# Attention values in one set of PSUM columns, and a softmax on negated scores

## The chip, the cores and the metric

One program on one core of a Trainium2 chip. The metric is the time of one execution on the device, in microseconds; lower is better. The core's engines work at the same time and wait for each other by semaphores: TensorE (PE) multiplies and writes to PSUM, VectorE (DVE) and ScalarE (ACT) compute on SBUF and PSUM, GpSimd (POOL) computes on SBUF and starts some transfers, SyncE (SP) starts the others.

## What is computed

One layer of an encoder, for a prompt of 2048 tokens and a sample of 8 x 16 tokens: a modulated RMS norm and a projection, a mixer of two halves (a gated delta rule, and attention in a band), an output projection and a feed-forward network. The change lies in the attention of the prompt, for 8 heads of width 64:

```
def one_chunk(c):                      # 64 queries, the 64 keys of their chunk and the 512 before them
    s = jnp.einsum('bqhd,bkhd->bhqk', qc, kc).astype(jnp.float32) * (DH ** -0.5) + bias
    p = jax.nn.softmax(jnp.where(valid, s, -jnp.inf), axis=-1).astype(v.dtype)
    return jnp.einsum('bhqk,bkhd->bqhd', p, vc)
```

and, in the softmax alone, in the attention of the sample.

## The kernel before

The kernel is written in a tile framework: the code says what is computed and in which buffers, pools hand out buffers of a tag in turn, and a scheduler sets the order of the instructions on each engine and their semaphores from the program as a whole. An edit in one place can so move instructions elsewhere.

Numbers are float32. For speed, the large matmuls run on fp32r operands; so that no accuracy is lost, an operand is split into two words, a high one (a rounded copy, by ACT) and a low one (the rest, by DVE or POOL), and their products are added. `mm3` (L160) does three matmuls for one product that way. The weights are cast by ACT (L175) and their low words made by POOL (L180) or loaded back from a store.

Phase 1 makes projections and the delta rule; the attention of token tiles 0 and 1 (`attention_first`) runs in it. Phase 2 takes the 16 token tiles and the sample tile in five blocks of 2, 4, 4, 4 and 3 tiles (`BLOCKS2`). For each block it runs `out_proj` (products `pso`), then `ffn`: 32 steps of `ffn_up` (products `psu`, L1480 to L1482; relu and square on ACT; the square again and the low word of `u` on DVE) and after every fourth the products `psd` with w_down, which DVE adds to `y`. While a block is in its FFN, the attention of the next block (`attention_gen`, L1212) is put in as filler: `tick` counts matmul columns and takes a step of the generator when enough have gone by.

A step of `attention_gen` handles a unit, one head of one tile of 128 queries, in three places of a pipeline. `scores` multiplies the queries (two words, `Qt`, stationary) with the keys into `psS`. `softmax_to` adds the bias and takes the maximum in one DVE pass (L1113), negates the maximum (L1114), takes the exponential with a running sum on ACT (L1115, listed at L92), inverts the sum (L1116) and scales (L1117). `probs` transposes the probabilities by PE into `psP` (L1275) and splits them into two words in `PT` (L1277): `PT[:, a, 0]` is the high word and `PT[:, a, 1]` the low one of key tile a. `values` multiplies: the stationary operand is `KV[:, w0 + a, 1]`, 128 keys by 128 columns, of which 64 are the high and 64 the low word of V; the moving one is `PT[:, a]`, both words side by side, 256 columns. The result `pv` has the words of V in its two halves of partitions and those of the probabilities in its two halves of columns; ACT copies the lower half of partitions to `otmp` (L1287), DVE adds the upper one (L1288) and then adds the two halves of columns to `of` (L1290; both adds are listed at L82), and SP stores `of` (L1292). `pv` has one buffer, which it shares with `pq`, the transposed queries of `prep_q` (L1250). A tile has 3, 4 or 5 key tiles; 112 units have 536 together.

Of the kernel before, what the change touches and what calls it, by code (L numbers as in the profile page):

```python
# [8 lines left out]
F32 = mybir.dt.float32  # L9
F32R = mybir.dt.float32r  # L10
AF = mybir.ActivationFunctionType
ALU = mybir.AluOpType
AX = mybir.AxisListType.X

P = 128
# [16 lines left out]
NEG = -1.0e30  # L32
# [19 lines left out]
class Trunk:  # L52
# [1056 lines left out]
    def softmax_to(self, s, ps, bias):  # L1109
        nc = self.nc  # L1110
        sv = s if len(ps.shape) == 2 else s.rearrange("p (z c) -> p z c", z=2)
        sm = self.small.tile([P, 4], F32, tag="sm", name="sm", bufs=4)
        nc.vector.tensor_tensor_reduce(sv, ps, bias, 1.0, NEG, ALU.add, ALU.max, sm[:, 0:1])  # L1113
        self.ts(sm[:, 1:2], sm[:, 0:1], -1.0, ALU.mult)  # L1114
        self.act(s, s, AF.Exp, bias=sm[:, 1:2], accum_out=sm[:, 2:3])  # L1115
        nc.vector.reciprocal(sm[:, 3:4], sm[:, 2:3])  # L1116
        self.ts(s, s, sm[:, 3:4], ALU.mult)  # L1117

# [93 lines left out]
    def attention_gen(self, tiles):  # L1212

        nc = self.nc
        mm = nc.tensor.matmul
# [4 lines left out]
        ap, ap2 = self.ap, self.ap2  # L1220
        heads, Q = {}, {}

        def psum(name):
            if name in ("pv", "pq"):
                return ap2.tile([P, 512], F32, tag="pv", name=name, bufs=4 - GP)
            return ap2.tile([P, 1024], F32, tag="att", name=name, bufs=2)
# [28 lines left out]
        def span(t):  # L1255
            lo_t = max(0, t - 4)
            return t + 1 - lo_t, lo_t - k0
# [22 lines left out]
        def values(h, t, PT):  # L1280
            m, w0 = span(t)
            KV = heads[h][0]
            pv = psum("pv")
            for a in range(m):
                mm(pv[:, 0:256].rearrange("p (z t) -> p z t", z=2), KV[:, w0 + a, 1], PT[:, a], start=(a == 0), stop=(a == m - 1))  # L1285
            tm = ap.tile([64, 256], F32, tag="otmp", name="otmp", bufs=2)
            nc.scalar.copy(tm, pv[64:128, 0:256])  # L1287
            self.tt(tm, tm, pv[0:64, 0:256], ALU.add)  # L1288
            o = ap.tile([64, P], F32, tag="of", name="of", bufs=2)
            self.tt(o, tm[:, 0:P], tm[:, P:256], ALU.add)  # L1290
            u = h % 2
            nc.sync.dma_start(self.s_ob[t][u * 64:(u + 1) * 64, h // 2], o)  # L1292

# [15 lines left out]
        pr, PT = {}, {}  # L1309
        for i in range(len(units) + 3):  # L1310
            if i >= 3:
                h, t = units[i - 3]
                values(h, t, PT.pop(i - 3))
                if t == tiles[-1]:
                    load_k(h + 2)
            if 2 <= i < len(units) + 2:
                PT[i - 2] = probs(*units[i - 2], pr.pop(i - 2))
            if i < len(units):
                h, t = units[i]
                pr[i] = scores(h, t)  # L1320
                if qs is not None:
                    prep_q(*qs)
                qs = next_q() if h % 2 and todo else None
            yield
# [267 lines left out]
```

## Time and profile before

| | us |
|---|---|
| median of the timed runs (3) | 3242.33 |
| lowest and highest of them | 3240.86, 3249.45 |
| profiled execution | 3235.24 |
| its span, from first to last instruction | 3233.5 |
| PE busy | 3071.4 (95%) |
| weight loads busy | 2713.0 (84%) |
| DVE busy | 1903.2 (59%) |
| ACT busy | 1478.5 (46%) |
| POOL busy | 701.2 (22%) |
| mean granted TensorE clock | 0.977 |

The clock is given as a share of 2.4 GHz; the granted level at any moment is that or half of it, 1.2 GHz. A matmul's row in the trace runs from its start to the modelled end of its results, so consecutive ones overlap: what one costs PE is the distance from its start to that of the next. A weight load (PEld) has a row of its own. The shares are means over stretches with different limits, so stretches are read apart.

### The profile page before, as it was taken

To read this page: it belongs to the slowest core of one execution; us is meant where nothing else is said; L and a number is where in the kernel's file an instruction comes from. 1 tells how busy PE (TensorE), PEld (TensorE's weight loads), DVE (VectorE), ACT (ScalarE), POOL (GpSimd) and SP (SyncE) were. 2 spreads that over 40 slices of the span, in tenths; PEclk is the share of its full clock that TensorE was granted. 3 is DMA by queue.
4 is the path that set the end of the run, shared out by engine and by line. 5 is a ranking of instruction groups with operands and counts; after the bars stand their busy time and mean duration, and the time that the engine had idled before them with its cause. 6 is when DMAs were issued, how large, how long until landed. Compare 5 with 4: busy or idle time off the path is not lost.

```text
span 3233.5 us, 53068 instructions
## 1 busy us (share of the span) xinstructions
PE 3071.4 (95%) x19577; PEld 2713.0 (84%) x19577; DVE 1903.2 (59%) x4526; ACT 1478.5 (46%) x2707; POOL 701.2 (22%) x561
## 2 busy tenths in 40 slices
PE   7899999999999979988999999999999999998998
PEld 6798988899989968878888889888888887787997
DVE  5985777777868676888446567235455443243223
ACT  3554544556656555554424444344434443333332
POOL 4641312121222347653343320000000000000000
PEclk9999999999989999998999999999999999998999
DMA  9789896878888765565565666665676667677875
GB/s 298 225 264 283 269 288 207 266 236 245 282 292 262 223 201 167 160 222 174 170 200 188 204 214 228 195 195 186 204 246 191 209 230 230 222 239 224 258 246 195
DMA packets 624507, 730.71 MB, mean 226 GB/s; under 512 B 59040, under 2 KB 483088, under 8 KB 622200
## 3 DMA queue, kind: packets, MB, share of 16 engines
q1 hardware_dynamic: 618488, 695.87, 68.0%
q0 software_dynamic: 5760, 31.46, 3.0%
q8 instruction: 154, 2.52, 0.3%
q14 instruction: 105, 0.86, 0.1%
HBM read 614.57 MB, written 115.52 MB: 226 GB/s over the span
## 4 chain that ended last, share of the span: by engine, by line
PE 71%; DVE 12%; DMA 9%; issue 3%; ACT 2%; SPq 1%; POOL 1%; POOLq 0%; DVEq 0%; ACTq 0%
PE psd L164 7%; PE psd L162 7%; PE psu L1480 7%; PE psu L1481 7%; PE psd L163 7%; PE psu L1482 7%; PE pv L1285 2%; PE psq L521 2%; PE psq L520 2%; PE psq L519 2%; PE psb L162 2%; PE psb L164 2%; PE psb L163 2%; PE psS L1267 2%; PE pso L162 2%
## 5 line engine op out<-in xcount | busy, mean ns | idle before, releaser
L175 ACT CAST w<-raw 128x1024 fp32r<-128x1024 f32 (+1 forms) x528 | 552.7, 1048 | 349.2 <-PE psd L164 163.2
L82 POOL TENSOR_TENSOR w<-raw,w 128x1024 fp32r<-128x1024 f32 (+1 forms) x172 | 418.3, 2443 | 365.8 <-ACT w L175 327.5
L1480 PE MATMUL psu<-hT,w 128*128 128x512 f32 (+2 forms) x1304 | 468.6, 361 | 7.1 <-ACT hT L104 6.2
L1481 PE MATMUL psu<-hT,w 128*128 128x512 f32 (+2 forms) x1304 | 467.2, 359 | 1.2 <-DVE hT L82 1.2
L1482 PE MATMUL psu<-hT,w 128*128 128x512 f32 (+2 forms) x1304 | 465.7, 357 | 0.0
L164 PE MATMUL psd<-w,u 128*128 128x512 f32 x1088 | 431.4, 398 | 9.1 <-DVE u L82 9.1
L162 PE MATMUL psd<-w,u 128*128 128x512 f32 x1088 | 432.5, 398 | 7.9 <-DVE y L82 4.1
L163 PE MATMUL psd<-w,u 128*128 128x512 f32 x1088 | 427.6, 393 | 0.0
L82 DVE TENSOR_TENSOR r<-r 128x512 f32<-128x512 f32 (+2 forms) x160 | 178.8, 1117 | 399.7 <-ACT u L92 399.4
L82 DVE TENSOR_TENSOR y<-y,psd 128x512 f32<-128x512 f32 x238 | 162.2, 684 | 242.0 <-PE psd L164 241.4
L1480 PEld LDWEIGHTS psu<-hT,w 128*128 128x128 f32 x1304 | 246.6, 190 | 39.8 <-ACT hT L104 7.4
L1481 PEld LDWEIGHTS psu<-hT,w 128*128 128x128 f32 x1304 | 246.8, 189 | 33.2 <-DVE hT L82 2.3
L1482 PEld LDWEIGHTS psu<-hT,w 128*128 128x128 f32 x1304 | 246.6, 189 | 32.5 <-issue 0.2
L92 ACT ACTIVATE r<-psu 128x512 f32<-128x512 f32 (+2 forms) x160 | 85.5, 534 | 408.7 <-PE psu L1482 349.6
L164 PEld LDWEIGHTS psd<-w,u 128*128 128x128 f32 x1088 | 204.9, 189 | 56.7 <-DVE u L82 10.4
L162 PEld LDWEIGHTS psd<-w,u 128*128 128x128 f32 x1088 | 205.3, 189 | 53.5 <-DVE y L82 6.7
L163 PEld LDWEIGHTS psd<-w,u 128*128 128x128 f32 x1088 | 205.6, 189 | 45.4 <-issue 1.0
L162 PE MATMUL psb<-w,hT 128*128 128x256 f32 x816 | 236.3, 290 | 0.7 <-ACT qraw L976 0.7
L164 PE MATMUL psb<-w,hT 128*128 128x256 f32 x816 | 234.1, 288 | 0.5 <-DVE hT L82 0.5
L163 PE MATMUL psb<-w,hT 128*128 128x256 f32 x816 | 233.4, 287 | 0.0
L520 PE MATMUL psq<-hT,w 128*128 128x384 f32 (+1 forms) x576 | 194.1, 337 | 0.0
L521 PE MATMUL psq<-hT,w 128*128 128x384 f32 (+1 forms) x576 | 193.9, 337 | 0.0
(318 smaller groups left out, 6603.0 us busy)
## 6 DMA issues: line engine op xcount, KB each, us to landing
raw<-in_w_up_dram SPq DMA_DIRECT2D x160, 512.0 KB
raw<-in_w_down_dram SPq DMA_DIRECT2D x160, 512.0 KB
raw<-in_w_in_dram SPq DMA_DIRECT2D x156, 512.0 KB
w<-s_w_in SPq DMA_DIRECT2D x130, 512.0 KB
w<-s_w_up SPq DMA_DIRECT2D x96, 512.0 KB
w<-s_w_down SPq DMA_DIRECT2D x96, 512.0 KB
raw<-in_w_out_dram SPq DMA_DIRECT2D x40, 512.0 KB
x<-in_x_prompt_dram SPq DMA_DIRECT2D x38, 512.0 KB
```

The lines of the kernel that those rows point to most:

```text
L82: (eng or self.nc.vector).tensor_tensor(out, in0, in1, op)
L92: self.nc.scalar.activation(out, in_, func, **kw)
L162: mm(out, lh, rh, start=first, stop=False)
L163: mm(out, lh, rl, start=False, stop=False)
L164: mm(out, ll, rh, start=False, stop=last)
L175: nc.scalar.copy(w[:, 0, 0:n], r)
L519: mm(ps[:, 0:T], wh, hT[:, k, 0, 0:T], start=(k == 0), stop=False)
L520: mm(ps[:, 0:T], wh, hT[:, k, 1, 0:T], start=False, stop=False)
L521: mm(ps[:, 0:T], wl, hT[:, k, 0, 0:T], start=False, stop=(k == KT - 1))
L1480: mm(ps[:, c0:c1], wh, h2[:, k, 0, c0:c1], start=(k == 0), stop=False)
L1481: mm(ps[:, c0:c1], wh, h2[:, k, 1, c0:c1], start=False, stop=False)
L1482: mm(ps[:, c0:c1], wl, h2[:, k, 0, c0:c1], start=False, stop=(k == KT - 1))
```

## The change

In `values` of `attention_gen`, the one matmul for each key tile, with both words of the probabilities side by side, becomes two with 128 columns each, which accumulate into the same 128 columns of `pv`. The add of the two halves of columns and the buffer `otmp` go; the ACT copy and the remaining DVE add have half the columns, and write to `of`. `attention_first` keeps its form.

In `softmax_to`, which all attention uses, the DVE pass stores the negated sum of score and bias and takes its minimum, which is the negated maximum. The exponential takes the scale -1 and that minimum as its bias, and the instruction that negated the maximum goes.

```
-        nc.vector.tensor_tensor_reduce(sv, ps, bias, 1.0, NEG, ALU.add, ALU.max, sm[:, 0:1])
-        self.ts(sm[:, 1:2], sm[:, 0:1], -1.0, ALU.mult)
-        self.act(s, s, AF.Exp, bias=sm[:, 1:2], accum_out=sm[:, 2:3])
+        nc.vector.tensor_tensor_reduce(sv, ps, bias, -1.0, -NEG, ALU.add, ALU.min, sm[:, 0:1])
+        self.act(s, s, AF.Exp, scale=-1.0, bias=sm[:, 0:1], accum_out=sm[:, 2:3])
...
             for a in range(m):
-                mm(pv[:, 0:256].rearrange("p (z t) -> p z t", z=2), KV[:, w0 + a, 1], PT[:, a], start=(a == 0), stop=(a == m - 1))
-            tm = ap.tile([64, 256], F32, tag="otmp", name="otmp", bufs=2)
-            nc.scalar.copy(tm, pv[64:128, 0:256])
-            self.tt(tm, tm, pv[0:64, 0:256], ALU.add)
+                for z in range(2):
+                    mm(pv[:, 0:P], KV[:, w0 + a, 1], PT[:, a, z], start=(a + z == 0), stop=(a == m - 1 and z == 1))
             o = ap.tile([64, P], F32, tag="of", name="of", bufs=2)
-            self.tt(o, tm[:, 0:P], tm[:, P:256], ALU.add)
+            nc.scalar.copy(o, pv[64:128, 0:P])
+            self.tt(o, o, pv[0:64, 0:P], ALU.add)
```

The scheduler writes a new order for both engines. On PE, among the products with w_down of a block with four tiles, a unit of five key tiles stood so before:

```order
L1285 MATMUL pv<-PT,KV 128x256 x5
L162 MATMUL psd<-w,u 128x512
L163 MATMUL psd<-w,u 128x512
L164 MATMUL psd<-w,u 128x512
L1275 MATMUL psP<-ident,sS 128x128 x5
L1267 MATMUL psS<-KV,Q 128x384 x2
L1267 MATMUL psS<-KV,Q 128x256 x2
```

and such a unit now, where lines after the removed one have a number lower by one:

```order
L1285 MATMUL pv<-PT,KV 128x128 x10
L1274 MATMUL psP<-ident,sS 128x128 x5
L1266 MATMUL psS<-KV,Q 128x384 x2
L1266 MATMUL psS<-KV,Q 128x256 x2
L162 MATMUL psd<-w,u 128x512
L163 MATMUL psd<-w,u 128x512
```

The ten narrow matmuls stand in a row, with no other matmul between the two of a pair. Of 112 units, 75 have ten in one row; in others the first stands apart by a few rows.

On DVE, in the FFN of the first block (two tiles), where the attention of tiles 2 to 5 is filled in, a unit's output and another's softmax stood so before (ISA is the pass with the maximum and the read of its result, `r` and `u` belong to the FFN):

```order
L82 TENSOR_TENSOR otmp<-otmp,pv 64x256
L1113 ISA sS,sm<-psS,bias 128x640
L1113 ISA sm 128x1
L82 TENSOR_TENSOR PT<-psP,PT 128x4x128
L82 TENSOR_TENSOR of<-otmp 64x128
L87 TENSOR_SCALAR sm<-sm 128x1
L1116 RECIPROCAL sm<-sm 128x1
L87 TENSOR_SCALAR sS<-sS,sm 128x640
```

and now:

```order
L82 TENSOR_TENSOR of<-of,pv 64x128
L1113 ISA sS,sm<-psS,bias 128x640
L1113 ISA sm 128x1
L82 TENSOR_TENSOR PT<-psP,PT 128x4x128
L82 TENSOR_TENSOR y<-y,psd 128x512
L1115 RECIPROCAL sm<-sm 128x1
L87 TENSOR_SCALAR sS<-sS,sm 128x640
```

The add from `otmp` and the negation are gone from between the maximum and the inverted sum, and an add to `y` has moved up into their place.

## Rows read from the trace of the kernel before

**Rows 1.** Busy time by stretch: length, PE, PEld, DVE, ACT, POOL, clock, DMA share, GB/s
```profile
1127.00:1187.00 60.00, 44.66 (x295) 40.34 (x296) 40.39 (x98) 30.03 (x58) 26.99 (x24) 0.86 0.71 232
1187.00:1439.00 252.00, 227.12 (x1467) 202.19 (x1466) 200.08 (x295) 137.99 (x252) 157.77 (x81) 0.98 0.56 169
1439.00:1529.00 90.00, 74.30 (x553) 70.96 (x552) 73.49 (x154) 40.57 (x77) 26.56 (x19) 0.88 0.59 191
1529.00:1941.00 412.00, 408.59 (x1981) 340.71 (x1980) 227.44 (x360) 169.34 (x278) 152.92 (x83) 0.99 0.61 197
...
1998.00:2413.00 415.00, 413.01 (x2027) 345.74 (x2028) 181.79 (x390) 178.63 (x296) 7.98 (x25) 1.00 0.62 199
...
2464.00:2627.00 163.00, 159.79 (x829) 135.32 (x830) 79.65 (x185) 81.39 (x144) 6.13 (x19) 0.98 0.65 208
```

**Rows 2.** The same for L1285 alone, the value product: length, PE, PEld, clock, DMA
```profile
1127.00:1187.00 60.00, 3.53 (x17) 2.65 (x17) 0.86 0.71 232
1187.00:1439.00 252.00, 17.10 (x102) 14.42 (x102) 0.98 0.56 169
1439.00:1529.00 90.00, 9.61 (x42) 7.66 (x42) 0.88 0.59 191
```

**Rows 3.** Timeline of PE, a unit among w_down's products: start, us, instruction
```profile
1706.28 0.40 PE L164 MATMUL psd<-w,u 128*128 128x512 f32 x1
1706.52 0.75 PE L1285 MATMUL pv<-PT,KV 128*128 128x256 f32 x5
1707.10 0.75 PE L1267 MATMUL psS<-KV,Q 128*128 128x384 f32 x4
```

**Rows 4.** Timeline of PE, scores of the first attention, two 128 and two 256
```profile
1023.38 0.62 PE L1163 MATMUL psS<-KV,Q 128*128 128x128 f32 x4
...
1023.72 0.28 PE L1163 MATMUL psS<-KV,Q 128*128 128x256 f32 x1
1023.84 0.28 PE L162 MATMUL psb<-w,hT 128*128 128x256 f32 x1
```

**Rows 5.** Groups of weight loads: shape, count, busy us, mean ns, idle before
```profile
L1481 PEld LDWEIGHTS psu<-hT,w 128*128 128x128 f32 x1304 | 246.8, 189 | 33.2 <-DVE hT L82 2.3 <-issue 0.8
L1285 PEld LDWEIGHTS pv<-PT,KV 128*128 128x128 f32 x536 | 80.1, 197 | 24.3 <-DVE otmp L82 7.0 <-DVE PT L82 6.0 <-ACT Q L1252 5.1
L1250 PEld LDWEIGHTS pq<-identr,qs 128*128 128x128 f32 x224 | 25.3, 145 | 16.7 <-DVE otmp L82 8.8 <-ACT qs L104 2.4 <-DVE qs L82 1.2
```

**Rows 6.** Timeline of PE, four fp32r transposes and the matmul behind them
```profile
926.28 0.45 PE L1011 MATMUL ptk<-identr,stk 128*128 128x128 f32 x4
926.58 0.35 PE L162 MATMUL psb<-w,hT 128*128 128x256 f32 x1
```

**Rows 7.** PE's waits in 1187 to 1439: total us, times, longest
```profile
PE psd L164 <- DVE u L82: 9.1, 3, 3.6
...
PE psS L1267 <- DVE sm L1113: 2.8, 3, 1.2
...
PE pv L1285 <- DVE otmp L82: 2.0, 2, 1.1
```

**Rows 8.** Groups of DVE in 1187 to 1439: count, busy us, mean ns, idle before
```profile
L82 DVE TENSOR_TENSOR of<-otmp 64x128 f32<-64x128 f32 x24 | 23.6, 985 | 0.2
...
L82 DVE TENSOR_TENSOR otmp<-otmp,pv 64x256 f32<-64x256 f32 x24 | 9.7, 406 | 2.8 <-ACT otmp L1287 2.8
...
L87 DVE TENSOR_SCALAR sm<-sm 128x1 f32<-128x1 f32 x23 | 3.3, 144 | 0.2
```

**Rows 9.** Timeline of DVE and of POOL beside it
```profile
1310.40 2.51 DVE L82 TENSOR_TENSOR of<-otmp 64x128 f32<-64x128 f32 x1
...
1310.35 2.40 POOL L82 TENSOR_TENSOR w<-raw,w 128x1024 fp32r<-128x1024 f32 x1
```

**Rows 10.** PE's waits in 1130 to 2640, two of the longest
```profile
PE pq L1250 <- DVE otmp L82: 7.7, 7, 2.2
PE psS L1267 <- DVE sm L1113: 6.1, 5, 2.3
```

## The prediction

> **What bounds the kernel now.** I read the table of busy time by stretch first, because the attention that the change touches (`attention_gen`) runs only from about 1140 to 2630 us, as a filler between the matmuls of out_proj and the FFN, and the limit is not the same all along [rows 1]. In 1529 to 1941, 1998 to 2413 and 2464 to 2627 TensorE (PE) is busy 408.6 of 412, 413.0 of 415 and 159.8 of 163 us at a granted clock of 0.98 to 1.00, that is at the 2.4 GHz level: there is no idle time that could take in more matmul work, and VectorE (DVE), at 181.8 of 415 us in one of them, has time to spare. In 1187 to 1439 it is otherwise: PE 227.1, DVE 200.1 and GpSimd (POOL) 157.8 of 252 us. What holds PE up there is seen in its waits in that stretch: most are for DVE, 9.1 us for `u`, 2.8 for `sm`, 2.0 for `otmp` [rows 7]. The two short stretches on either side, 1127 to 1187 and 1439 to 1529, hold the out_proj of two blocks beside attention units; PE idles 15 and 16 us in them [rows 1].
>
> So the change has to be priced twice: what it costs PE, which is paid in full where PE is the limit, and what it gives back on DVE and ScalarE (ACT), which counts only where PE waits for them.
>
> **What the change does to PE.** There are 536 matmuls of the value product [rows 5], 256 moving columns each [rows 3]. A unit with five key tiles takes from 1706.52 to 1707.10 us, 0.116 us each, at full clock [rows 3]. Afterwards there are 1072 of 128 columns, back to back, ten to a unit, as the order shows. The columns are as many as before, so if streaming were all, nothing would change. But each matmul here brings its own weight load, also where the next one has the same stationary operand: L1481 takes the same `wh` as L1480, and still has 1304 loads for 1304 matmuls [rows 5]. I expect no load to be saved by the pair with the same `KV`.
>
> What two loads per 256 columns cost is read where 128-column matmuls in fp32r already stand: the scores of the first attention, L1163. Four of them, two of 128 and two of 256 columns, begin at 1023.38, the last at 1023.72, and the next matmul begins at 1023.84 [rows 4]. They take 0.46 us; the two of 256 columns are 0.234 of that at the rate above, which leaves 0.226 for the two of 128, 0.113 each, hardly less than a 256-column one. The load, not the stream, sets the pace. From the other side: if a load were as quick as that of the fp32r transposes, four of which take 0.30 us (926.28 to 926.58), the price would be 0.075 each [rows 6]. I take 0.111 to 0.113, since the value product's loads last 197 ns in the mean and those of the transposes at L1250 145 ns [rows 5]: `KV` is loaded in the slower way. A pair then costs 2 x 0.112 - 0.116 = 0.108 us more than the single matmul it replaces.
>
> Of the 536, 17 lie in 1127 to 1187, 102 in 1187 to 1439 and 42 in 1439 to 1529 [rows 2]; the other 375 in the stretches where PE is the limit or next to it. There the price is paid in full: 375 x 0.108 = +40.5 us. The 161 early ones add 17.4 us of PE work, of which some may go into idle time.
>
> By the Trainium skill (TensorE: Matmul & The Clock Gate, Back-to-back issue gap) a sustained stream of loads and matmuls of 128 columns runs at about 81 ns each; by that, an estimate, the 375 would cost 375 x (0.162 - 0.116) = 17 us and not 40. The same sentence gives 131 ns for 512 columns, which this trace does not bear out (the 512-column matmul ahead of that unit holds PE for 0.24 us, from 1706.28 to 1706.52 [rows 3]), so I hold to the rows.
>
> **What it gives back on DVE and ACT.** Per unit two adds of DVE go, `otmp` with `pv` (64x256) and `of` from `otmp` (64x128), and one add of 64x128 with `pv` comes. The negation of the maximum, a 128x1 instruction of 0.144 us, goes. In 1187 to 1439 the 24 units spent 23.6 us on `of`, 9.7 on `otmp` and 3.3 on `sm` [rows 8]. The `of` add is dear there, 0.985 us in the mean, because it can stand still beside POOL: at 1310.40 it lasts 2.51 us while a POOL subtraction runs from 1310.35 for 2.40 us [rows 9]. It reads both operands from SBUF; the `otmp` add, with one operand in PSUM, lasts 0.406 us there, and the new add is of this second kind. Its price lies below the 0.406 of twice the columns; I take 0.3 and bound it by 0.2 and 0.41. So DVE gets back 36.6 - 24 x 0.3 = 29 us of its 200 in this stretch. The `sm` step also stood behind that `of`, in the chain to the exponential.
>
> The ACT copy of 64x256 becomes one of 64x128. It now writes `of` itself, so it is ACT that waits if the store of two units before has not landed, and behind it on ACT stand the weight casts L175 and the relu L1484. Two units are some 20 us apart in 1187 to 1439 (24 units in 252 us), so I cost that wait at nothing; if several units are drained in a row it can be a microsecond each. Reducing with min in place of max, and the scale of -1 in the exponential, replace operands in instructions that are there anyway; I cost them at nothing. A bound for it: if the reduction took a tenth longer it would be on DVE, which has time where PE is the limit.
>
> **Where the relief counts.** In 1187 to 1439 PE idles 25 us, of which some 16 are for DVE: the three of [rows 7] and four smaller ones. With 29 us of DVE work gone from 24 units I take these 16 as gone, against 102 x 0.108 = 11.0 of new PE work: -5 us. Bounds: +11, if the waits stay, and -14, if all 25 go. Over the whole attention the waits for `otmp` and `sm` are led by 7.7 us (L1250) and 6.1 us (L1267) [rows 10], and about 16 us of them lie outside 1187 to 1439. A unit's way from `pv` to a free buffer becomes shorter by some 0.2 us there, and DVE's queue by half a microsecond, so I take half of them, 8 us; 6 in the two out_proj stretches, which pay 59 x 0.108 = 6.4 for their new PE work, and 2 later.
>
> **The sum.** 40.5 - 2 (stretches at PE's limit) - 5 (1187 to 1439) + 0 (out_proj stretches) = +33.5 us. The early part, before 1127, has 16 softmaxes with one small DVE step less, and the sample's attention after 2627 eight; PE does not wait for those, nothing. The profiled execution took 3235.24 us for a span of 3233.5; it lies 7 us below the median of the timed runs, 3242.33, and I carry the difference over to that: 3242.3 + 33.5 = 3275.8, about +1.0%. Bounds from the same terms: no relief at all, 57.9 us, 3300; the most of it (-14, -4 and -8 in place of -5, -2 and 0), some +14, 3257. The scheduler also writes much of the rest in another order, which may move it by a few microseconds either way.
>
> **The rivals.** First, *the relief does not come*: what waits for DVE now waits a little later for ACT or for POOL's weights. For it: POOL is busy 158 of 252 us in that stretch and is not touched. Against: the waits name DVE. +57.9, 3300. Second, *the clock falls*: the bursts of load-bound matmuls keep the array half idle, and rows of the stretches with many waits show a granted clock of 0.86 and 0.88, that is, part of the time at 1.2 GHz [rows 1]. If the 990 us at PE's limit went from 0.99 to 0.97, that is +20: 3296. Against: transposes, which are bursts of the same kind, stand there now, at 0.98 to 1.00. Third, *the loads go as fast as those of the transposes*, 0.075 each, a pair 0.034 above the single matmul: 375 x 0.034 - 2 in the late stretches, 102 x 0.034 - 16 in 1187 to 1439, 59 x 0.034 - 6 beside it, together -6 us, 3236, no change to be measured. By the skill's 81 ns, an estimate, the same three come to about +1, 3243. Against: [rows 4], which is the same type and shape at 0.113. Fourth, on the other side, *the second load of a pair costs nothing*, because it brings the same weights: then PE's work stays as it was and the relief is left, -16 - 8 = -24, 3218, faster. The point from which it decides is a price of a pair under 24 / 536 = 0.045 us above the single one. Against: the same-weight pair at L1480 and L1481 has its loads, and the loads of L1163 are as long.
>
> **How the numbers follow.** Forecast, 3257 to 3300 with 3276 as the likeliest: 0.70. No relief: 0.11. Clock: 0.06. Quick loads: 0.08. Free second load: 0.05. The range 3253 to 3302 leaves out the last two and the far end of the clock case. A measurement of this kernel can tell about 0.3%, 9.7 us, from no change. Faster by more than that: 0.05, the fourth rival. Within it: 0.10, the third and a little of the forecast's lower end. Slower: 0.85.
>
> **What would show it.** In the profile after, the 1072 value matmuls should begin 0.11 us apart, a unit of ten taking about 1.1 us in place of 0.58, and the three late stretches should be longer by about 0.108 us for each pair, 15 us for the one with 135. The `of` add should show no instance of 2 us, DVE's busy time should fall by 60 to 90 us in all, and PE's waits for `otmp` should be fewer. I am wrong if the matmuls of 128 columns stand at 0.06 to 0.08 us, if the late stretches grow by more than the value product does, or if the stretch at 1187 grows by 11 us although DVE has fewer things to do.

## The result and the profile after

The changed kernel takes 3283.47 us in the median of four runs (3281.44 to 3292.17) against 3241.60: a ratio of 1.0131, with a 95% interval of 1.0109 to 1.0152. Timed once more, in six runs on another occasion, it is at 1.0085 (1.0064 to 1.0105). The two intervals do not overlap; both say slower, by 42 us and by 26 us in the medians. The forecast was 3276, or 1.0103.

The profiled execution took 3285.28 us, span 3283.6. Busy: PE 3134.9 us (before 3071.4), DVE 1834.6 (1903.2), ACT 1471.9 (1478.5), POOL 701.3 (701.2). DVE's fall of 69 us lies in the 60 to 90 that were forecast. By stretch, cut at the same points of the program as [rows 1] (length, PE, PEld, DVE, ACT, POOL, clock, DMA share, GB/s):

```profile
1137.00:1204.00 67.00, 50.19 (x345) 45.78 (x346) 49.13 (x100) 34.94 (x71) 27.30 (x19) 0.87 0.70 223
1204.00:1452.00 248.00, 236.35 (x1566) 213.99 (x1566) 172.32 (x245) 136.27 (x247) 156.22 (x81) 0.97 0.55 167
1452.00:1533.00 81.00, 71.96 (x539) 69.74 (x538) 60.19 (x113) 31.33 (x59) 23.83 (x15) 0.89 0.55 184
1533.00:1960.00 427.00, 422.50 (x2130) 355.64 (x2131) 216.83 (x322) 170.58 (x284) 157.09 (x85) 1.00 0.61 197
2016.00:2453.00 437.00, 430.84 (x2175) 362.86 (x2174) 170.35 (x333) 176.68 (x295) 7.20 (x23) 0.99 0.60 191
```

Against [rows 1], the two long stretches at PE's limit grew from 412 to 427 and from 415 to 437 us; the first FFN stretch shrank from 252 to 248 and the out_proj behind it from 90 to 81, while the out_proj ahead of it grew from 60 to 67. In the first FFN stretch PE's busy time rose from 227 to 236 us and its idle time fell from 25 to 12, and DVE's busy time fell from 200 to 172, by 28 us where 29 were forecast. The first column of PE counts shows the narrow matmuls coming in: 1566 against 1467 in the first FFN, 2130 against 1981 in the second.

One unit among w_down's products, in the timeline of PE (start, us, instruction), answers [rows 3]:

```profile
1729.83 0.39 PE L163 MATMUL psd<-w,u 128*128 128x512 f32 x1
1730.06 1.23 PE L1285 MATMUL pv<-PT,KV 128*128 128x128 f32 x10
1731.12 0.45 PE L164 MATMUL psd<-w,u 128*128 128x512 f32 x1
1731.41 0.40 PE L162 MATMUL psd<-w,u 128*128 128x512 f32 x1
```

Ten matmuls of 128 columns take 1.06 us, 0.106 each; the five of 256 columns took 0.58. The matmul of 512 columns behind the ten is longer for it: it holds PE for 0.29 us, from 1731.12 to 1731.41, where the one ahead of them took 0.23. With these 0.06 the ten cost 1.12 us, 0.112 each. No load is saved by the pair with the same `KV`, as this group of weight loads shows (count, busy us, mean ns, idle before), which answers [rows 5]:

```profile
L1285 PEld LDWEIGHTS pv<-PT,KV 128*128 128x128 f32 x1072 | 139.3, 195 | 18.6 <-ACT Q L1251 5.5 <-DVE PT L82 2.5 <-DVE of L82 2.4
```

The other half, DVE's relief, is there as well. The add to `of` no longer stands still beside POOL (minimum, median, maximum in ns; before 262/279/2699), and PE's waits for DVE in the first FFN stretch add up to 9.1 us (6.5 in the second profile) where all of before, those of [rows 7] and the smaller ones, were 16.3. Those behind the value product's own output, `otmp` before and `of` now, did not become shorter there: 4.7 us and 2.5, against 2.2. The four longest waits of the first profile:

```profile
L82 DVE TENSOR_TENSOR of<-of,pv x112: 258/275/281, 1175.8 to 2666.3; 64x128 f32<-64x128 f32 x112
```

```profile
PE psd L164 <- DVE u L82: 3.8, 3, 1.6
PE pq L1249 <- DVE of L82: 2.8, 2, 1.6
PE psS L1266 <- DMA KV<-s_kv: 2.3, 1, 2.3
PE pv L1285 <- DVE of L82: 1.9, 1, 1.9
```

Why do the two timings differ? A part is the clock, which also differs before 913 us, where PE's order of instructions is that of before: in the first profile of the changed kernel the granted clock there is 0.96, in the second 0.98 (before 0.97). Over the whole span it stood at 1.2 GHz for 181 us of the first profile, 158 of the second and 154 of the one before; since 1.2 GHz is half of the other level, 23 us more of it cost up to 11.5 of the 15.8 us between the two profiles. The timed runs say the same: their mean granted clocks average 0.974 in the first timing and 0.977 in the second, where the runs of before beside it have 0.972. So the second ratio may be too good, and whether the change itself raises the clock was not tested. The first out_proj starts at 1137 and 1134 us, before at 1127; two profiles of one kernel, f_three below, differ there as much, 1138 and 1127, so this is no cost of the change. In the second profile the stretches that the change touches are alike, 243, 428 and 433 us for the three FFN stretches:

```profile
0.00:913.00 913.00, 853.73 (x6459) 784.88 (x6460) 673.40 (x1965) 464.86 (x945) 261.50 (x244) 0.96 0.84 260
```

```profile
0.00:913.00 913.00, 850.14 (x6511) 782.08 (x6512) 677.77 (x1976) 470.32 (x954) 263.83 (x249) 0.98 0.84 263
1202.00:1445.00 243.00, 234.23 (x1564) 213.10 (x1564) 168.55 (x242) 135.28 (x244) 156.45 (x81) 0.98 0.55 169
1525.00:1953.00 428.00, 423.17 (x2128) 356.12 (x2127) 214.42 (x319) 170.35 (x284) 156.16 (x85) 0.99 0.60 196
2009.00:2442.00 433.00, 428.00 (x2180) 360.68 (x2179) 170.62 (x333) 176.81 (x296) 7.21 (x23) 1.00 0.61 193
```

### The profile page after: what moved, and what is told of

It reads as the page before. It is cut to its first block, busy times and chain, and to the rows that moved or that the text cites. A ratio compares the mean times of both kernels' runs of the same rounds, so it can differ in the third digit from the quotient of the medians.

```text
span 3283.6 us, 53983 instructions
## 1 busy us (share of the span) xinstructions
PE 3134.9 (95%) x20113; PEld 2780.6 (85%) x20113; DVE 1834.6 (56%) x4278; ACT 1471.9 (45%) x2707; POOL 701.3 (21%) x561
## 4 chain that ended last, share of the span: by engine, by line
PE 72%; DMA 11%; DVE 9%; issue 2%; ACT 2%; SPq 1%; POOL 1%; POOLq 0%; ACTq 0%; DVEq 0%
PE psu L1478 7%; PE psd L164 7%; PE psu L1479 7%; PE psd L162 7%; PE psu L1480 7%; PE psd L163 7%; PE pv L1285 3%; PE psS L1266 2%; PE psq L521 2%; PE psq L520 2%; PE psq L519 2%; PE psb L162 2%; PE psb L163 2%; PE psb L164 2%; PE pso L162 1%
```

## Experiments

| kernel | ratio to before | 95% interval |
|---|---|---|
| the change, first and second timing | 1.0131, 1.0085 | 1.0109 to 1.0152, 1.0064 to 1.0105 |
| softmax alone (a_softmax) | 0.9973 | 0.9960 to 0.9987 |
| value product alone (b_values) | 1.0103 | 1.0083 to 1.0123 |
| pairs for tiles 2 to 5 (d_early) | 0.9982 | 0.9966 to 0.9998 |
| pairs for tiles 6 to 15 (c_late) | 1.0105 | 1.0085 to 1.0125 |
| same loads, half the columns (e_half) | 1.0098 | 1.0072 to 1.0123 |
| half the loads and columns (e_onehigh) | 0.9924 | 0.9902 to 0.9946 |
| narrow between wide (g_mixed) | 1.0100 | 1.0073 to 1.0128 |
| wide matmul, last add a reduction (f_reduce) | 0.9973 | 0.9954 to 0.9992 |
| wide matmul, three quarters (f_three, twice) | 1.0016, 1.0014 | 0.9999 to 1.0034, 1.0002 to 1.0026 |
| the same, four buffers of `of` (f_three_of4) | 0.9999 | 0.9987 to 1.0011 |

### Which half of the change loses, and where

The softmax alone is the first part of the diff, the value product alone the second. All the other kernels have the new softmax. For d_early and c_late the old and the new form of `values` stand side by side; c_late has `>=`:

```
+            if tiles[0] < 6:
+                for a in range(m):
+                    for z in range(2):
+                        mm(pv[:, 0:P], KV[:, w0 + a, 1], PT[:, a, z], start=(a + z == 0), stop=(a == m - 1 and z == 1))
...
+            else:
+                for a in range(m):
+                    mm(pv[:, 0:256].rearrange("p (z t) -> p z t", z=2), KV[:, w0 + a, 1], PT[:, a], start=(a == 0), stop=(a == m - 1))
...
```

> The negated softmax alone, the value product as before. Theory (the loss is the second weight load of each pair in the value product): PE's work is that of before, DVE has 128 steps of 0.144 us less, most of them where PE is the limit. Expected -6 to +2 us against before, 3235 to 3244; each late stretch as long as before. Rival (the loss comes from the scheduler's new order, which the softmax alone sets off, since the profile after shows its first stretch, up to the first out_proj, 10 us longer although the value product is not in it): +8 to +20 us, with that first stretch 10 us longer here too.

> The value product in pairs of 128 columns alone, the softmax as before. Theory of the second weight load: the whole of the loss is here, +38 to +48 us, with the late stretches longer as after the full change (about 15, 16 to 22 and 6 to 9 us) and weight loads twice as many at the value product. Rival (order set off by the softmax): +20 to +30 at most.

> The pairs for tiles 2 to 5 alone, whose attention is filled into the first FFN block, where DVE and POOL are busy; tiles 6 to 15 keep the matmul with 256 columns; the new softmax everywhere. Theory (the price is paid where PE is the limit, and the DVE relief outweighs it where PE waits for DVE): -14 to +3 us, 3227 to 3245, with the stretch of the first FFN 4 to 10 us shorter than the 252 of before and the later ones unchanged. Rival (the relief does not count, and the 136 pairs there cost 0.108 us each as elsewhere): +10 to +17 us, 3252 to 3259.

> The pairs for tiles 6 to 15 alone (400 of the 536 key tiles of the value product, in the stretches where PE has no idle time), the matmul of before for tiles 2 to 5, the new softmax everywhere. Theory (each pair costs one more load, 0.098 to 0.108 us, and nothing in these stretches gives it back): 39 to 43 us on top of the softmax alone (-9 us), +28 to +38 us, a ratio of 1.0085 to 1.012, with the late FFN stretches as long as after the full change (427, 437, 443) and the first one as with the softmax alone (243). Rival (half of the loss is in the early part, where a unit's chain from pv to its output grew): +12 to +22 us.

The softmax alone gains 0.27% (9 us), more than the -6 to +2 that was expected. Its first FFN stretch is 242 us long, but also holds fewer matmuls than that of [rows 1], 1434 against 1467, with 222 against 227 us of PE work:

```profile
1198.00:1440.00 242.00, 221.60 (x1434) 198.79 (x1433) 179.65 (x256) 133.28 (x237) 155.71 (x79) 0.98 0.55 169
```

Its timed runs have a mean granted clock of 0.9765, the runs of before beside them 0.9731. That is some 22 us less at 1.2 GHz, worth up to 11 us, as much as the whole gain. Whether the shorter chain keeps the clock up or the 9 us have another cause is not shown. The value product alone is at 1.0103, a loss of 33 us, under the expected 38 to 48 and over the rival's 20 to 30. So the loss is not from a new order set off by the softmax. Split by place, the pairs of tiles 2 to 5 (136 of 536) leave the kernel at 0.9982, the pairs of tiles 6 to 15 (400) at 1.0105. d_early's profile shows both halves of the theory: the first FFN stretch (second line) has 1564 matmuls in place of 1467 and is 244 us long, not 252; the later ones are within 3 us of before, 415 and 417:

```profile
1136.00:1205.00 69.00, 53.64 (x346) 49.83 (x347) 51.71 (x102) 35.63 (x73) 27.06 (x19) 0.81 0.67 216
1205.00:1449.00 244.00, 235.05 (x1564) 213.35 (x1563) 173.99 (x242) 135.50 (x245) 156.23 (x81) 0.98 0.56 168
1449.00:1530.00 81.00, 70.28 (x523) 67.75 (x521) 62.60 (x119) 31.97 (x60) 24.63 (x15) 0.89 0.56 188
1530.00:1945.00 415.00, 409.43 (x1989) 340.80 (x1990) 229.75 (x350) 174.95 (x288) 154.97 (x85) 1.00 0.63 203
2002.00:2419.00 417.00, 413.16 (x2019) 346.03 (x2020) 180.40 (x363) 177.64 (x296) 7.40 (x25) 0.99 0.62 198
```

and c_late the reverse, 242 and then 430 and 436 (against a_softmax, 1.32% or 43 us for its 400 pairs, 0.107 each):

```profile
1204.00:1446.00 242.00, 222.64 (x1439) 199.28 (x1439) 181.31 (x257) 133.64 (x239) 156.42 (x79) 0.98 0.56 170
1532.00:1962.00 430.00, 425.97 (x2117) 358.74 (x2118) 216.28 (x316) 170.11 (x282) 157.02 (x84) 0.98 0.61 197
2018.00:2454.00 436.00, 429.67 (x2173) 362.05 (x2171) 169.78 (x332) 176.15 (x295) 7.21 (x23) 0.99 0.60 191
```

> The full change once more, timed in more rounds on the same chip as the run beside it. If the sum of the parts holds (softmax alone 0.9973, value product alone 1.0103) it is at 1.0065 to 1.0105, +21 to +34 us, and the 1.0131 of the first four runs was partly the clock, which stood at half for 181 us of the profiled execution against 154 before. If it is at 1.011 to 1.015 again, the two parts together cost something that neither does alone, some 10 to 17 us.

The parts multiply to 0.9973 x 1.0103 = 1.0076; the second timing of the whole, 1.0085, agrees, the first does not. By the second, nothing is left that only both parts together would cost; with intervals of 0.2% to either side, some 7 us could hide.

### Loads or columns

e_half keeps every load and halves the columns. It leaves out the products of 64 of the 128 queries; its copy and add read each column twice (not shown in the cut), so that they keep their size:

```
-                    mm(pv[:, 0:P], KV[:, w0 + a, 1], PT[:, a, z], start=(a + z == 0), stop=(a == m - 1 and z == 1))
+                    mm(pv[:, 0:64], KV[:, w0 + a, 1], PT[:, a, z, 0:64], start=(a + z == 0), stop=(a == m - 1 and z == 1))
...
```

> The full change with half of each value matmul left out: the pairs multiply 64 queries in place of 128 (the other 64 get a copy of the first half's result), so there are 1072 matmuls with the same 1072 weight loads and half of the columns; copy and add keep their size. Theory (the load sets the pace): spacing stays at 0.11 us and the time at that of the full change, 3272 to 3290. Rival (the pace is set by the columns streamed, or by accumulating into the same columns right after one another): spacing near 0.06 and about 1072 x 0.05 x 0.7 = 37 us less, 3240 to 3252.

e_onehigh halves both: it leaves out the low words of the probabilities, and so has as many columns as e_half and half of its loads:

```
-                for z in range(2):
-                    mm(pv[:, 0:P], KV[:, w0 + a, 1], PT[:, a, z], start=(a + z == 0), stop=(a == m - 1 and z == 1))
+                mm(pv[:, 0:P], KV[:, w0 + a, 1], PT[:, a, 0], start=(a == 0), stop=(a == m - 1))
```

> The full change with the low words of the probabilities left out of the value product: 536 matmuls of 128 columns in place of 536 of 256, copy, add and softmax as after the change. Theory (a matmul costs what its weight load costs, 0.11 us, as long as its columns take less): PE's work is that of before although half the columns are gone, spacing 0.11; the late stretches are within 4 us of before (412, 415), and what is left is the relief on DVE and ACT with the 9 us of the softmax alone: -10 to -28 us, a ratio of 0.991 to 0.997. Rival (columns count): spacing 0.06, the late stretches 6 to 9 us shorter each, -35 to -50 us.

With half of the columns gone, e_half is at 1.0098, inside the interval of the second timing of the change; its second FFN stretch is 427 us long, as after the change. Ten matmuls of 64 columns take 1.03 us, and the one behind them 0.32 in place of 0.23, so that the ten cost 1.12 us as well:

```profile
1530.00:1957.00 427.00, 422.07 (x2125) 355.18 (x2126) 213.91 (x318) 168.25 (x281) 154.89 (x84) 1.00 0.60 195
1762.23 1.20 PE L1285 MATMUL pv<-PT,KV 128*128 128x64 f32 x10
1763.26 0.48 PE L1481 MATMUL psu<-hT,w 128*128 128x512 f32 x1
1763.58 0.39 PE L1479 MATMUL psu<-hT,w 128*128 128x512 f32 x1
```

With half of the loads gone too, e_onehigh falls to 0.9924, 22 us faster than before in its own pair of medians (3221.13 against 3242.99). Its late stretches are as before, 411 and 415 us, and the first FFN stretch is 230:

```profile
1204.00:1434.00 230.00, 219.90 (x1441) 198.53 (x1441) 169.31 (x237) 132.63 (x239) 156.13 (x81) 0.98 0.59 179
1514.00:1925.00 411.00, 407.59 (x1989) 339.88 (x1989) 220.07 (x320) 171.16 (x286) 154.14 (x84) 0.99 0.63 204
1985.00:2400.00 415.00, 412.52 (x2026) 344.69 (x2025) 166.13 (x326) 174.62 (x295) 7.32 (x25) 0.99 0.61 195
```

Between e_onehigh and e_half, with the same columns and twice the loads, lie 1.0098 - 0.9924 = 1.74%, 56 us, for 536 loads: 0.105 us for each. From the second timing of the change it is 1.61%, 52 us, 0.097 for each; from the first, 2.07%, 67 us, 0.125. This is the price of the second load, a mean over all stretches, against the 0.108 of the prediction. The rival in which columns count is out.

### Can the loads be hidden by the order?

In g_mixed the narrow matmuls of a unit are written between the wide ones of another unit's scores; the unit's copy and add then come behind these scores. In part:

```
             for (a, b) in segs:
                 for z in range(2):
                     mm(ps[:, c0 + a * P:c0 + b * P], Qt[:, z, h % 2], KV[:, w0 + a:w0 + b, 0],
                        start=(z == 0), stop=(z == 1))
+                    wide -= 1
+                    while narrow and len(narrow) > wide * left // (len(segs) * 2):
+                        narrow.pop(0)()
```

> The full change, with the value matmuls of a unit written between the wide matmuls of another unit's scores (384 and 256 columns); by the order some 55 of 112 units come out mixed, two or three narrow matmuls behind each wide one. Theory (a load can begin when the matmul before has begun, so a matmul costs the longer of its load, 0.11 us, and its columns): a wide neighbour hides one load and no more, which it does for its own, so the narrow ones still cost 0.11 on average and the time is that of the full change within 8 us, 3274 to 3292. Rival (loads queue up behind wide matmuls and are hidden by them): a mixed unit gains 0.1 to 0.25 us, late stretches 4 to 8 us shorter than after the change in all, and narrow matmuls behind wide ones at 0.06.

It is at 1.0100. The timeline of PE in a mixed unit shows why nothing is gained:

```profile
1752.97 0.34 PE L1268 MATMUL psS<-KV,Q 128*128 128x384 f32 x1
1753.15 0.45 PE L1288 MATMUL pv<-PT,KV 128*128 128x128 f32 x3
1753.44 0.39 PE L1268 MATMUL psS<-KV,Q 128*128 128x384 f32 x1
1753.66 0.33 PE L1288 MATMUL pv<-PT,KV 128*128 128x128 f32 x2
1753.84 0.33 PE L1268 MATMUL psS<-KV,Q 128*128 128x256 f32 x1
1754.01 0.45 PE L1288 MATMUL pv<-PT,KV 128*128 128x128 f32 x3
1754.29 0.33 PE L1268 MATMUL psS<-KV,Q 128*128 128x256 f32 x1
1754.45 0.33 PE L1288 MATMUL pv<-PT,KV 128*128 128x128 f32 x2
1754.62 0.73 PE L1279 MATMUL psP<-ident,sS 128*128 128x128 f32 x5
```

Two narrow ones behind a wide one take 0.18 and 0.17 us and three take 0.29 or 0.28, less than 0.11 each: the first goes quickly, since its load was done beside the wide one. But the next wide one pays it back: 384 columns take 0.18 us at 1752.97, behind another wide matmul, and 0.22 at 1753.44, behind narrow ones; 256 columns take 0.17 and 0.16 in place of the 0.116 of [rows 3]. The unit as a whole, ten narrow and four wide, takes 1754.62 - 1752.97 = 1.65 us, and so do, to 0.01 us, all 22 units of its trace that stand in this order; apart they were 1.06 and, by [rows 3] and the start of the matmul behind it, some 0.59. This is what comes out if each matmul costs the longer of its load, 0.11, and its columns, so that a load is hidden by one matmul ahead and no more. It also speaks against another rival, that a matmul waits for the one before it because both add to the same columns of `pv`: here four of the ten, and not only the first, stand behind a wide matmul that adds to other columns, and the unit is no shorter.

### What the relief consists of

f_reduce keeps the value product of before and changes only its last add (the first two lines). f_three keeps the matmul of before and puts the output together from three quarters of `pv`, leaving out the product of the two low words (the last three lines):

```
-            self.tt(o, tm[:, 0:P], tm[:, P:256], ALU.add)
+            nc.vector.tensor_reduce(o.unsqueeze(2), tm.rearrange("p (z t) -> p t z", z=2), AX, ALU.add)
...
+            nc.scalar.copy(o, pv[64:128, 0:P])
+            self.tt(o, o, pv[0:64, 0:P], ALU.add)
+            self.tt(o, o, pv[0:64, P:256], ALU.add)
```

> The softmax of the change, and the value product and its copy and first add as before; only the last add, of two halves of otmp, both in SBUF, is a reduction of one operand, so it has one input instead of two. Theory (the add with two operands in SBUF stands still while POOL runs, and that is what PE waits for): the output step never lasts 2 us, is 0.3 to 0.45 us long, and the first FFN stretch is a few us shorter than with the softmax alone (242.6): ratio 0.993 to 0.997. Rival (it stands in nobody's way): as the softmax alone, 0.996 to 0.999.

> The softmax of the change, and the matmul of before with 256 columns and one weight load for each key tile; the output is put together without the product of the two low words, which mm3 leaves out too: ACT copies 64x128, DVE adds two quarters of pv, each with one operand in PSUM, 0.28 us each. Theory (the loss is the second load, the gain is the DVE work that goes, above all the add that stands still beside POOL): no loss in the late stretches, the first FFN stretch 8 to 14 us and the second out_proj up to 8 us shorter than the 252 and 90 of before; -10 to -25 us, 0.992 to 0.997. Rival (the gain is that of the softmax alone): 0.996 to 0.999, no different from the 0.9973 measured for that.

The reduction does not stand still, 0.414 us in the mean where the add took 0.985 [rows 8]. But f_reduce is at 0.9973, the same as the softmax alone, so the rival's reading holds: this stall alone was in nobody's way. Where its time went is less clear. The difference `u` of the FFN, which also reads two operands from SBUF and can last 2.5 us, is longer there. Its group in the first FFN stretch, in f_reduce and then in a_softmax (busy us, mean ns):

```profile
L82 DVE TENSOR_TENSOR u<-r,u 128x256 fp32r<-128x256 f32 x32 | 42.4, 1324 | 1.1
...
L1289 DVE TENSOR_REDUCE of<-otmp 64x128 f32<-64x256 f32 x22 | 9.1, 414 | 0.2
```

```profile
L82 DVE TENSOR_TENSOR u<-r,u 128x256 fp32r<-128x256 f32 x32 | 36.0, 1126 | 1.1
L82 DVE TENSOR_TENSOR of<-otmp 64x128 f32<-64x128 f32 x22 | 17.5, 796 | 0.2
```

Of the 8.4 us that the reduction saves there, `u` takes 6.4. That the stall goes from one instruction to the other is not shown by this, though: `u` was as long before, beside an add that did stand still, and is as short after the change, whose add does not (before, then after):

```profile
L82 DVE TENSOR_TENSOR u<-r,u 128x256 fp32r<-128x256 f32 x32 | 41.9, 1309 | 1.1
```

```profile
L82 DVE TENSOR_TENSOR u<-r,u 128x256 fp32r<-128x256 f32 x32 | 35.7, 1115 | 1.1
```

f_three missed: expected at 0.992 to 0.997, it came out at 1.0016 and, timed again, 1.0014. Its first FFN stretch is shorter, but in the out_proj behind it PE waits for the one `pv` buffer. The timeline of ACT and of PE there (in brackets the idle time before, and for what):

```profile
1464.18 0.26 ACT L1286 COPY of<-pv 64x128 f32<-64x128 f32 x1 [5.41 <-DMA s_ob<-of]
```

```profile
1465.21 1.19 PE L1284 MATMUL pv<-PT,KV 128*128 128x256 f32 x4 [7.17 <-DVE of L82]
```

The ACT copy, which now writes `of` itself, waits 5.41 us until the store of an earlier unit has landed; the adds wait for the copy, and PE for the adds. That is the wait that the prediction had costed at nothing. In the changed kernel's own profiles the copy does not wait for a store, so there the term was right. To see what it was worth, `of` got four buffers, and the old form ran again beside it:

```
-            o = ap.tile([64, P], F32, tag="of", name="of", bufs=2)
+            o = ap.tile([64, P], F32, tag="of", name="of", bufs=4)
```

> The kernel f_three (256 columns, one load, output from three quarters of pv without the product of the two low words) with four buffers for of in place of two, so that the ACT copy that now writes of does not wait for the store of two units before. Theory (f_three lost its gain in the second out_proj, where the copy waited 5.4 us for a store and PE 7.2 us behind it for the one pv buffer): the out_proj stretch of 91.5 us becomes 80 to 84, the wait for the store is gone, and the ratio falls from 1.0016 to 0.9955 to 0.9985. Rival (that wait was one instance, and the second add on pv holds the buffer in every unit): 0.9995 to 1.003, with PE's waits for of elsewhere as long as before.

> The same kernel as f_three once more on the same chip as the run with four buffers: 1.000 to 1.003 by its first twelve runs; if it comes out at 0.998 or below, the first result was partly the clock and the difference to the run beside it is what counts.

PE's wait for `of` at the value product falls from 11.5 us (7.6 the longest) to 3.6 (2.5), f_three_again first:

```profile
PE pv L1284 <- DVE of L82: 11.5, 3, 7.6
```

```profile
PE pv L1284 <- DVE of L82: 3.6, 2, 2.5
```

The copy itself still waits for a store once, 3.7 us in place of 5.9 (f_three_again first), and the out_proj stretch is 88 us long in place of 90, not the expected 80 to 84:

```profile
ACT of L1286 <- DMA s_ob<-of: 5.9, 1, 5.9
```

```profile
ACT of L1286 <- DMA s_ob<-of: 3.7, 1, 3.7
```

The ratio goes from 1.0014 to 0.9999, about 5 us, or 2 us in the medians; the intervals overlap (1.0002 to 1.0026, 0.9987 to 1.0011), so it is not settled by the times alone. It stays above the 0.9973 of the softmax alone, of which f_three also has the whole. The expected 0.9955 to 0.9985 was not reached; the result lies in the range of the rival, 0.9995 to 1.003, in which that wait was one instance. Where the remaining 8 us are is open, and that a second add on `pv` holds its only buffer longer is argued, not shown.

## Why the prediction was right, point by point

**The limit by stretch.** It was read from [rows 1] and holds: the same edit is nearly free where PE waits for DVE (0.9982 for d_early, against 0.9973 without pairs) and cost in full where PE does not wait (1.0105 for c_late).

**The price of a pair.** It was worked out as 0.108 us from four matmuls of another line, [rows 4]. The spacing measured afterwards is 0.106 in a unit of ten, or 0.112 with what the matmul behind the ten is longer, and the difference of e_half and e_onehigh gives 0.105 for each load. The 536 pairs were put at 57.9 us; by that difference they cost 56. The rival with loads as quick as the transposes' is out. Its 0.075 was itself read too low, since the matmul of 256 columns behind the four transposes of [rows 6] holds PE from 926.58 to 926.76, 0.06 longer than 0.116: with these 0.06 they cost 0.09 each. By the Trainium skill (TensorE: Matmul & The Clock Gate, Back-to-back issue gap) 128 columns would be at about 81 ns each. This trace does not agree: they stand at 106, and 64 columns at 103. The second load of the same weights is not free either: 1072 loads for 1072 matmuls.

**The relief.** It was put at 24 us in all, 16 of them in the first FFN stretch, where all waits for DVE were taken as gone. The size is about right. In that stretch PE's idle time fell from 25 us to 12, and to 9 in the second profile, by 13 and 16. Not all of it is what was named: the waits for DVE fell only from 16.3 to 9.1 and 6.5 us, and the rest is that PE's waits for ACT there, 6.3 us before, are gone. In total, e_onehigh, which has the new softmax, copy and add but one load for each key tile, is 0.76% faster, 25 us, with the gain in the first FFN stretch (230 us) and the out_proj behind it (80); that its total meets the 24 is in part luck, since its matmuls are a little shorter as well, 0.11 us each in place of 0.116. The split was off. The softmax, which was given nothing of its own, brings 9 us, by what way is open; what the shorter copy and adds bring, together with matmuls of half the columns, is the difference to 25. The reason named, the `of` add that stands still beside POOL, is not shown to be what counts: taking away this stall alone, in f_reduce, gained nothing over the softmax. The first FFN stretch came out at 248 and 243 us against a forecast of 247. The two out_proj stretches, forecast as unchanged in sum, went from 60 and 90 us to 67 and 81, 148 in place of 150, with seven pairs more in the first and twelve fewer in the second.

**The late stretches.** They were to grow by 0.108 us a pair. The first has 140 pairs where before it had 135 matmuls of the value product; it grew from 412 to 427 and 428 us, where 15.1 was due for 140. The next, with 150 pairs and 16.2 us due, grew from 415 to 437 and 433; the 6 us more in the first profile and 2 in the second stand beside a wait for `y` of 3.0 and 2.1 us, which before had none there. The third can be compared only up to the end of the program, because its end was cut at another place: from its start it is 769.5 us before, 776.6 and 773.8 after, where 75 pairs were to cost 8. Taken together, from the start of the second FFN stretch (1529, 1533 and 1525 us) to the end, the program grew from 1704.5 to 1750.6 and 1742.8 us: 46 and 38, for a forecast of 40.5 - 2 = 38.5. This is the main term of the sum, and it holds, to the few us by which single profiles differ (that of before lay 7 us below its median).

**The clock.** A fall in the late stretches was a rival; the granted clock there is 0.99 to 1.00, as before. It moved elsewhere, also where nothing was changed, before 913 us, and accounts for a part of the difference between the two timings of one kernel.

**The rival on the other side** needed a pair to cost under 0.045 us; it costs more than twice that.

## What to carry to other kernels

Before a matmul is cut into narrower ones, look for a narrow one of the same type and read the distance to its neighbour: if it is not shorter in proportion, as here, each cut costs a load, and two words side by side in the moving operand can be worth a later add on DVE. The price has to be put against the stretch in which it falls; here the same edit is nearly free in one and costs 15 us in the next. A stall is not time gained when it goes: f_reduce took one of 2.7 us at its longest away and was no faster. And the granted clocks of two sets of runs should be put side by side before a difference of some 10 us is given a cause.

## What the runs showed of the hardware that was not expected

A narrow matmul behind a wide one looks cheap in the timeline, and the wide one behind it is longer for it: 256 columns took 0.16 to 0.17 us there in place of 0.116. Read alone, the first of the two misleads. And the smallest edit of the diff, which takes one DVE instruction of 0.144 us out of each unit, was worth 9 us in a kernel in which DVE is busy 59% of the time. It may be that it stood in a chain that PE waits for in the one stretch where DVE is short of time; the clock of those runs was higher too, and the two were not separated.
